# Low-rank products on all rows, a block-diagonal chunk map and shared PSUM banks in the second mixer of a hybrid decoder step

## The chip, the cores and the metric

The kernel runs on one core of a Trainium2 chip. The metric is the device time of one execution in microseconds (us); less is better. The engines are TensorE (PE in the profile; PEld is its weight load), VectorE (DVE), ScalarE (ACT), GpSimd (POOL) and SyncE (SP), whose queue issues the DMAs.

## What is computed

One decoder layer for 512 prompt tokens and 8 x 8 sample tokens (576 columns), all in float32: a first mixer (mLSTM, 4 heads), a second mixer (RWKV-7, 8 heads of 64, in 4 pairs), gates that merge both, a convolutional feed-forward block and a gated embedding. The change lies in the second mixer:

```python
wlog = -jax.nn.softplus(-(lp['r_w0'] + jnp.tanh(wd) @ lp['r_w2'])) - 0.5
decay = jnp.exp(-jnp.exp(wlog.astype(f32)))
a = jax.nn.sigmoid(lp['r_a0'] + ad @ lp['r_a2'])
...
def step(S, inp):
    rt, wt, kt, vt, at, bt = inp
    sa = jnp.einsum('bhij,bhj->bhi', S, at)
    S = S * wt[:, :, None, :] + sa[..., None] * bt[:, :, None, :] + vt[..., None] * kt[:, :, None, :]
    return S, jnp.einsum('bhij,bhj->bhi', S, rt)
```

The kernel computes this recurrence in chunks of 64 tokens: within a chunk by matrix products, and from chunk to chunk by a map of the 64x64 state of each head.

## The kernel before

Activations lie with channels on the 128 partitions and the 576 tokens as columns, in two halves of 288. A dense product (`dense`, L171; its matmul is L190) splits each weight and each activation into a high and a low float32r part and adds three products, so one output tile of 8 input tiles is 2 x 24 matmuls of 128 rows, 128 columns and 288 moving columns. Weights come by `wload` (L158): a DMA from SP into one of 6 staging buffers (L165), a cast on ACT (L166) and a subtraction on DVE (L167) into one of 4 pairs of buffers `wh`, `wl`. A float32r matmul or a transpose leaves one record in the trace, a float32 matmul two.

`PLAN` lists the steps of the two mixers: for each head pair p of the second mixer `rwkv_in` (projections), `rwkv_prep` (L550), `rwkv_mid` (L723), `rwkv_smp` (L839) and `rwkv_out` (L882); the mLSTM heads (`mlstm_head`, L1062); and 16 gate tiles (`gate`). A scheduler then interleaves the instructions of all of these on each engine, with priorities by program order and by a model of times, and writes one fixed order per engine. Each engine takes its order strictly, so a change of a few instructions moves others too. PSUM banks come by tags: "d" (3 banks) for the dense products, "r" (2), "s" (1), "c" (1) and "m" (1) for the mixers.

In the second mixer, per head pair:

- `rwkv_prep` makes decay and gate from two low-rank products, each from a 64-row input. `xw` and `xa` hold 128 rows: the rounded input on one half, its remainder on the other. For each half of the columns and each of the two, L566 multiplies all 128 rows by the rounded weights and L567 the 64 rounded rows by the weights' remainder (`lh`).
- `rwkv_mid` solves the chunks and makes, with 64-row matmuls from one "s" bank at a time: the output within the chunk (L806, a bank for each head), the read maps `Rt` (L817, a bank for each parity of the chunks), the state additions `Ns` (L824), and the transition maps `MT` (L835, again a bank for each parity; L836 adds the identity).
- `rwkv_smp` handles the sample tokens. The values of one head are multiplied with a mask of the 8 sequences (`UVM`, L874, one buffer) and go through one matmul of 512 columns (L876), then the other head.
- `rwkv_out` runs the chain over the chunks: 7 steps, each with two 64x64 matmuls (L902), one for each head on its half of the partitions, and one DVE operation (L903), then the outputs (L909).

After the mixers come the branch products (`gated`, L1229; second mixer's branch first), whose result `mg` goes through w_out. Seven of its eight output tiles have their weights staged by three buffers of their own into `oh`, `ol`; the memory of these tiles is shared with earlier pools.

Of the kernel before, what the change touches and what calls it, by code (L numbers as in the profile page):

```python
# [7 lines left out]
F32 = mybir.dt.float32  # L8
F32R = mybir.dt.float32r
AF = mybir.ActivationFunctionType  # L10
ALU = mybir.AluOpType
# [4 lines left out]
P = 128  # L16
D = 1024
TP = 512
NB = 8
TS = 8  # L20
T = TP + NB * TS
HF = T // 2
# [70 lines left out]
def build(tc, nc, I, O):  # L93
    from contextlib import ExitStack

    V, S, G, TE, SY = nc.vector, nc.scalar, nc.gpsimd, nc.tensor, nc.sync
# [9 lines left out]
    with st0:  # L106
# [263 lines left out]
        with ExitStack() as stn:  # L370
# [156 lines left out]
        NPP = 1  # L527
# [12 lines left out]
            return t.rearrange("g (b x) -> g b x", x=1040)[:, :, 0:1024].rearrange("g b (s y) -> g b s y", y=64)[:, :, :, 0:16]  # L540

        WP = [zeroed(rp, [P, 592], f"WP_{i}", 1.0) for i in range(NPP)]
        YT = [zeroed(rp, [P, 5, P], f"YT_{i}") for i in range(NPP)]

        pairs = [{} for _ in range(4)]
# [4 lines left out]
        def rwkv_prep(p):  # L550
            xr, xk, xv = pairs[p]["x"]
            lr = rp.tile([P, 2, P], F32, tag="t4", name="lr")
            SY.dma_start(lr, I["lora_wa"][:, p])
            lh = rp.tile([P, 3, P], F32R, tag="t5", name="lh")
            S.copy(lh[:, 0:2, :], lr)
            for i in range(2):
                r = slice(64 * i, 64 * i + 64)
                V.tensor_tensor(lh[r, 2, :], lr[r, i, :], lh[r, i, :], ALU.subtract)
            sp = rp.tile([P, T], F32, tag="t1", name="sp")
            tha = rp.tile([P, T], F32, tag="t3", name="tha")  # L560
            for hf in range(2):
                c = slice(hf * HF, (hf + 1) * HF)
                pw, pa = bank("r"), bank("r")
                for i, (pm, x) in enumerate(((pw, xw), (pa, xa))):
                    r = slice(64 * i, 64 * i + 64)
                    TE.matmul(pm[:, 0:HF], lh[:, i, :], x[:, c], start=True, stop=False)  # L566
                    TE.matmul(pm[:, 0:HF], lh[r, 2, :], x[r, c], start=False, stop=True)  # L567
                S.activation(sp[:, c], pw[:, 0:HF], AF.Tanh, bias=hw0[:, p:p + 1], scale=0.5)
                S.activation(tha[:, c], pa[:, 0:HF], AF.Tanh, bias=ha0[:, p:p + 1], scale=0.5)
            V.tensor_scalar(sp, sp, 1.0, None, ALU.add)  # L570
# [16 lines left out]
            pm = bank("r")  # L587
# [131 lines left out]
        def slots(t, inner):  # L719
            a = t[:, 0:1024].rearrange("p (i s x) -> p i s x", i=4, s=4)  # L720
            return (a[:, :, 1:3, :] if inner else a[:, :, 0:4:3, :]), t[:, 1024 + 64 * inner:1024 + 64 * inner + 64]

        def rwkv_mid(p):  # L723
# [74 lines left out]
                V.tensor_copy(At[:, 4 * h:4 * h + 4, :], pu[:, :, 64:128])  # L798

            Y = YT[0]  # L800
            for h in range(2):
                f = slice(64 * h, 64 * h + 64)
                py = bank("s").rearrange("p (i x) -> p i x", i=8)
                for i in range(4):
                    for par in range(2):
                        TE.matmul(py[64 * par:64 * par + 64, i, :], (G0, G1)[par][:, h, i, 64 * par:64 * par + 64], UV[:, 2 * i + par, f], start=True, stop=True)  # L806
                V.tensor_copy(Y[:, 0:4, f], py[:, 0:4, :])
            RT_ = rp.tile([P, 8, 64], F32, tag="Rt", name="Rt")
            RTv = RT_.rearrange("p (i q) x -> p i q x", i=4)
            Rv = slots(AR, 0)[0]  # L810
            for par in range(2):
                b = 64 * (1 - par)
                pm = bank("s").rearrange("p (c x) -> p c x", c=8)
                for i in range(4):
                    for h in range(2):
                        f = slice(64 * h, 64 * h + 64)
                        TE.matmul(pm[f, i, :], At[b:b + 64, 4 * h + i, :], (G0, G1)[par][b:b + 64, h, i, 64 - b:128 - b], start=True, stop=True)  # L817
                V.tensor_tensor(RTv[:, :, par, :], pm[:, 0:4, :], Rv[:, :, par, :], ALU.add)
            WL = wl[:, 0:8].unsqueeze(2).to_broadcast([P, 8, 64])
            pn = bank("s").rearrange("p (c x) -> p c x", c=8)  # L820
            for c in range(8):
# [5 lines left out]
            MT = rp.tile([P, 8, 64], F32, tag="MT", name="MT")  # L827
            MTv = MT.rearrange("p (i q) x -> p i q x", i=4)
            for par in range(2):
                b = 64 * (1 - par)  # L830
                pm = bank("s").rearrange("p (c x) -> p c x", c=8)
                for i in range(4):
                    for h in range(2):
                        f = slice(64 * h, 64 * h + 64)
                        TE.matmul(pm[f, i, :], At[b:b + 64, 4 * h + i, :], BT[b:b + 64, 2 * i + par, f], start=True, stop=True)  # L835
                V.tensor_tensor(MTv[:, :, par, :], pm[:, 0:4, :], cc("ident2", 64).unsqueeze(1).to_broadcast([P, 4, 64]), ALU.add)  # L836
            pairs[p].update(MT=MT, Ns=Ns, RT=RT_, Q4=Q4)

        def rwkv_smp(p):  # L839

            AR, wl, G4, B8, U8, Q4 = (pairs[p][n] for n in ("AR", "wl", "G4", "B8", "U8", "Q4"))
            Y4 = rp.tile([64, P], F32, tag="Y4", name="Y4", bufs=2)
            S0C = rp.tile([P, NB, 64], F32, tag="S0C", name="S0C")
            SY.dma_start(S0C, I["st_S"][p])
            pa = bank("r")
            arv = AR[:, 1024:1152].rearrange("p (s b x) -> p b s x", s=2, b=NB)
            for b in range(NB):
                for h in range(2):
# [12 lines left out]
            for h in range(2):  # L861
                f = slice(64 * h, 64 * h + 64)
                TE.matmul(pu[64:128, f], Q4[64:128, h, :], Xs[64:128, f], start=True, stop=True)
            S.copy(U8[64:128, :], pu[64:128, :])
            py = bank("r")[:, 0:P]
            for h in range(2):
                f = slice(64 * h, 64 * h + 64)
                TE.matmul(py[0:64, f], G4[:, h, 0:64], U8[:, f], start=True, stop=True)
            V.tensor_tensor(Y4, py[0:64, :], Xs[0:64, :], ALU.add)
            pS = bank("r")  # L870
            for h in range(2):
                f = slice(64 * h, 64 * h + 64)
                UVM = rp.tile([P, NB, 64], F32, tag="UVM", name="UVM")
                V.tensor_tensor(UVM, U8[:, f].unsqueeze(1).to_broadcast([P, NB, 64]),  # L874
                                cc("bmask", 8).unsqueeze(2).to_broadcast([P, NB, 64]), ALU.mult)
                TE.matmul(pS[f, :], B8[:, f], UVM, start=True, stop=True)  # L876
            V.tensor_tensor(S0C, S0C, pS.rearrange("p (b x) -> p b x", b=NB), ALU.add)
            V.tensor_tensor(S0C, S0C, wl[:, 8:16].unsqueeze(2).to_broadcast([P, NB, 64]), ALU.mult)
            SY.dma_start(O["o_S_s"][p], S0C)
            pairs[p]["Y4"] = Y4  # L880

        def rwkv_out(p):  # L882
# [14 lines left out]
            V.tensor_copy(Sa[:, 1, :], Ns[:, 0, :])  # L897
            for c in range(1, 8):
                pS = bank("c")
                for h in range(2):  # L900
                    f = slice(64 * h, 64 * h + 64)
                    TE.matmul(pS[f, 0:64], MT[f, c, :], Sa[f, c, :], start=True, stop=True)  # L902
                V.scalar_tensor_tensor(Sa[:, c + 1, :], pS[:, 0:64], wl[:, c:c + 1], Ns[:, c, :], ALU.mult, ALU.add)  # L903
            SY.dma_start(O["o_S_p"][p], Sa[:, 8, :])
            for h in range(2):
# [607 lines left out]
```

## Time and profile before

| | |
|---|---|
| median of 3 runs | 1110.08 us (1108.51 to 1112.6) |
| the profiled execution's own time | 1105.56 us |
| its span, first to last instruction | 1103.9 us |
| granted TensorE clock over the span | 0.995 of full |
| DMA moved | 114.54 MB, 104 GB/s in the mean |

The page gives busy times by engine, the stretches the same by time, and the timeline the start of each matmul. A matmul's duration includes its way through the array, and the next one starts before it ends; the time that it takes from PE's queue is the distance to the next start. Line numbers are those of the kernel before; the kernel after has its own, at most 8 away from these.

### The profile page before, as it was taken

How to read it: one execution, taken by the hardware profiler on the slowest of the kernel's cores; microseconds unless marked ns; L12 is line 12 of the kernel's file. 1: busy time of each engine (PE TensorE's matmuls, PEld its weight loads, DVE VectorE, ACT ScalarE, POOL GpSimd, SP SyncE). 2: the span in 40 equal slices, each digit the busy share in tenths (PEclk: the TensorE clock that was granted, in tenths of full speed). 3: DMA queues.
4: the chain of work that ended last, by engine and by line, in shares of the span. 5: the costliest groups of instructions: out<-in, count | busy, mean ns of one | idle time of the engine just before them, and what ended most of it. 6: DMA issues, size and time to landing. Idle time of an engine off the chain costs nothing. (4 is left out here: it accounts for less than half of the span.)

```text
span 1103.9 us, 23247 instructions
## 1 busy us (share of the span) xinstructions
PE 1075.5 (97%) x9039; PEld 1014.2 (92%) x9039; DVE 785.3 (71%) x1690; ACT 509.2 (46%) x1075; POOL 254.6 (23%) x401
## 2 busy tenths in 40 slices
PE   6899999999999999999989999999999999999997
PEld 5899989989979888898989999999999999999997
DVE  7786756766757667346693799974899569976765
ACT  6584733453435244325241556541455335553732
POOL 6532112220112022002130152410144103510300
PEclk9999999999999999999999999999999999999999
DMA  6343412332342232427780212332223332242414
GB/s 220 96 123 92 105 51 55 97 119 65 93 133 80 75 82 85 141 80 235 231 276 1 69 44 87 96 100 93 77 86 95 93 92 87 84 122 64 147 48 132
DMA packets 90799, 114.54 MB, mean 104 GB/s; under 512 B 35612, under 2 KB 45212, under 8 KB 90688
## 3 DMA queue, kind: packets, MB, share of 16 engines
q1 hardware_dynamic: 90688, 113.05, 34.2%
q8 instruction: 71, 1.16, 0.4%
q14 instruction: 40, 0.33, 0.1%
HBM read 94.57 MB, written 18.45 MB: 102 GB/s over the span
## 5 line engine op out<-in xcount | busy, mean ns | idle before, releaser
L166 ACT CAST wh<-wr 128x512 fp32r<-128x512 f32 (+2 forms) x170 | 101.6, 599 | 198.4 <-PE pd L190 157.3
L167 DVE TENSOR_TENSOR wl<-wr,wh 128x512 fp32r<-128x512 f32 (+2 forms) x170 | 119.7, 707 | 81.2 <-ACT wh L166 78.3
L190 PE MATMUL pd<-actl,wh 128*128 128x288 f32 x384 | 111.9, 295 | 0.0
L190 PE MATMUL pd<-acth,wl 128*128 128x288 f32 x384 | 111.4, 295 | 0.0
L190 PE MATMUL pd<-acth,wh 128*128 128x288 f32 x384 | 110.4, 296 | 0.5 <-ACT pp L1376 0.5
L190 PEld LDWEIGHTS pd<-acth,wh 128*128 128x128 f32 x384 | 71.1, 188 | 0.8 <-ACT pp L1376 0.7
L190 PEld LDWEIGHTS pd<-actl,wh 128*128 128x128 f32 x384 | 71.8, 188 | 0.0
L190 PEld LDWEIGHTS pd<-acth,wl 128*128 128x128 f32 x384 | 71.6, 188 | 0.0
L288 ACT CAST wh<-ws 128x512 fp32r<-128x512 f32 x76 | 47.0, 619 | 47.6 <-PE pd L300 26.8
L289 DVE TENSOR_TENSOR wl<-ws,wh 128x512 fp32r<-128x512 f32 x76 | 59.0, 777 | 8.2 <-ACT wh L288 7.9
L294 POOL TENSOR_TENSOR ws<-wr 128x512 f32<-128x512 f32 x19 | 31.9, 1682 | 93.6 <-DVE wl L289 53.1
L1326 POOL COPY o_f<-u 128x2 f32<-128x2 f32 x22 | 26.6, 1208 | 110.5 <-DVE u L1323 108.8
L288 ACT CAST wh<-wr 128x512 fp32r<-128x512 f32 x57 | 35.3, 619 | 35.0 <-PE pd L300 21.1
L289 DVE TENSOR_TENSOR wl<-wr,wh 128x512 fp32r<-128x512 f32 x57 | 39.6, 694 | 7.3 <-ACT wh L288 7.2
L1335 DVE SCALAR_TENSOR_TENSOR y<-u,vec,y 128x592 f32<-128x592 f32 x44 | 38.0, 863 | 1.4 <-ACT y L1333 1.3
L207 POOL TENSOR_TENSOR rsc<-rsc,nhalf 128x3 f32<-128x3 f32 x8 | 7.3, 912 | 137.0 <-DVE rsc L229 137.0
L247 ACT ACTIVATE sq<-res 128x288 f32<-128x288 f32 x40 | 17.7, 444 | 45.8 <-DVE res L1272 27.2
L190 PE MATMUL pd<-mgl,oh 128*128 128x288 f32 x112 | 33.1, 296 | 0.0
L190 PE MATMUL pd<-mgh,ol 128*128 128x288 f32 x112 | 33.1, 295 | 0.0
L190 PE MATMUL pd<-mgh,oh 128*128 128x288 f32 x112 | 32.8, 295 | 0.0
L1363 DVE TENSOR_TENSOR res<-res,pd 128x288 f32<-128x288 f32 x48 | 20.9, 451 | 15.6 <-PE pd L190 15.5
L190 PE MATMUL pd<-xa0h,wh 128*128 128x288 f32 x86 | 26.6, 310 | 2.1 <-ACT zr L346 2.0
(820 smaller groups left out, 3979.2 us busy)
## 6 DMA issues: line engine op xcount, KB each, us to landing
wr<-i_w_in SPq DMA_DIRECT2D x92, 256.0 KB
wr<-i_f_up SPq DMA_DIRECT2D x88, 256.0 KB
wr<-i_f_down SPq DMA_DIRECT2D x32, 256.0 KB
d_th<-gst SPq DMA_DIRECT2D x16, 288.0 KB
th<-d_th SPq DMA_DIRECT2D x16, 288.0 KB
wr<-i_w_br SPq DMA_DIRECT2D x16, 256.0 KB
wr<-i_w_out SPq DMA_DIRECT2D x16, 256.0 KB
wr<-i_ple_gate SPq DMA_DIRECT2D x16, 256.0 KB
```

The costliest lines, as they stand in the source:

```text
L166: S.copy(wh[:, 0:nk, :], wr[:, 0:nk, :])
L167: V.tensor_tensor(wl[:, 0:nk, :], wr[:, 0:nk, :], wh[:, 0:nk, :], ALU.subtract)
L190: TE.matmul(pm[:, 0:HF], w[:, k % 4, :], a[:, c], start=k == 0 and i == 0, stop=k == n - 1 and i == 2)
L207: G.tensor_tensor(t, t, nhalf[0:t.shape[0], :].to_broadcast([t.shape[0], n]), ALU.pow)
L247: S.activation(sq, x[:, c], AF.Square)
L288: S.copy(wh, w)
L289: V.tensor_tensor(wl, w, wh, ALU.subtract)
L294: e.tensor_tensor(t, a, b, ALU.add)
L1326: G.tensor_copy(o_f[:, j, 0:2], u[:, TP:TP + 2])
L1335: V.scalar_tensor_tensor(y, u[:, i:i + 592], w(i), y, ALU.mult, ALU.add)
L1363: V.tensor_tensor(x1[m][:, c], x1[m][:, c], pss[hf][:, 0:HF], ALU.add)
```

## The change

In `rwkv_prep` the weights' remainder is kept on all 128 rows for both products, and the second matmul of a pair multiplies all 128 rows. In `rwkv_mid` the outputs of both heads go to one bank and leave it in one copy; read and transition maps of one parity share a bank, and the transition maps land in `MTP`, a tile zeroed once, one head's 64x64 map in the upper left and the other's in the lower right of each chunk's 128x128 block. `rwkv_out` then needs one matmul per step. In `rwkv_smp` the mask is applied to both heads in one operation.

```diff
+        MTP = [zeroed(rp, [P, 8, P], f"MT_{i}") for i in range(NPP)]
...
-            lh = rp.tile([P, 3, P], F32R, tag="t5", name="lh")
+            lh = rp.tile([P, 4, P], F32R, tag="t5", name="lh")
             S.copy(lh[:, 0:2, :], lr)
-            for i in range(2):
-                r = slice(64 * i, 64 * i + 64)
-                V.tensor_tensor(lh[r, 2, :], lr[r, i, :], lh[r, i, :], ALU.subtract)
+            V.tensor_tensor(lh[:, 2:4, :], lr, lh[:, 0:2, :], ALU.subtract)
...
                     TE.matmul(pm[:, 0:HF], lh[:, i, :], x[:, c], start=True, stop=False)
-                    TE.matmul(pm[:, 0:HF], lh[r, 2, :], x[r, c], start=False, stop=True)
+                    TE.matmul(pm[:, 0:HF], lh[:, 2 + i, :], x[:, c], start=False, stop=True)
...
+            py = bank("s").rearrange("p (h i x) -> p h i x", h=2, i=4)
             for h in range(2):
                 f = slice(64 * h, 64 * h + 64)
-                py = bank("s").rearrange("p (i x) -> p i x", i=8)
...
-                V.tensor_copy(Y[:, 0:4, f], py[:, 0:4, :])
+            V.tensor_copy(Y[:, 0:4, :].rearrange("p i (h x) -> p h i x", h=2), py)
...
             for par in range(2):
                 b = 64 * (1 - par)
-                pm = bank("s").rearrange("p (c x) -> p c x", c=8)
-                for i in range(4):
-                    for h in range(2):
-                        f = slice(64 * h, 64 * h + 64)
-                        TE.matmul(pm[f, i, :], At[b:b + 64, 4 * h + i, :], (G0, G1)[par][b:b + 64, h, i, 64 - b:128 - b], start=True, stop=True)
-                V.tensor_tensor(RTv[:, :, par, :], pm[:, 0:4, :], Rv[:, :, par, :], ALU.add)
+                pm = bank("s").rearrange("p (q i x) -> p q i x", q=2, i=4)
+                for q, rhs in enumerate((lambda h, i: (G0, G1)[par][b:b + 64, h, i, 64 - b:128 - b],
+                                         lambda h, i: BT[b:b + 64, 2 * i + par, 64 * h:64 * h + 64])):
+                    for i in range(4):
+                        for h in range(2):
+                            TE.matmul(pm[64 * h:64 * h + 64, q, i, :], At[b:b + 64, 4 * h + i, :], rhs(h, i), start=True, stop=True)
+                V.tensor_tensor(RTv[:, :, par, :], pm[:, 0], Rv[:, :, par, :], ALU.add)
+                for h in range(2):
+                    f = slice(64 * h, 64 * h + 64)
+                    V.tensor_tensor(MTv[f, :, par, f], pm[f, 1], cc("ident2", 64)[f].unsqueeze(1).to_broadcast([64, 4, 64]), ALU.add)
...
+            UVM = rp.tile([P, NB, P], F32, tag="UVM", name="UVM")
+            V.tensor_tensor(UVM, U8.unsqueeze(1).to_broadcast([P, NB, P]), cc("bmask", 8).unsqueeze(2).to_broadcast([P, NB, P]), ALU.mult)
             for h in range(2):
                 f = slice(64 * h, 64 * h + 64)
-                UVM = rp.tile([P, NB, 64], F32, tag="UVM", name="UVM")
...
-                TE.matmul(pS[f, :], B8[:, f], UVM, start=True, stop=True)
+                TE.matmul(pS[f, :], B8[:, f], UVM[:, :, f], start=True, stop=True)
...
             for c in range(1, 8):
                 pS = bank("c")
-                for h in range(2):
-                    f = slice(64 * h, 64 * h + 64)
-                    TE.matmul(pS[f, 0:64], MT[f, c, :], Sa[f, c, :], start=True, stop=True)
+                TE.matmul(pS[:, 0:64], MT[:, c, :], Sa[:, c, :], start=True, stop=True)
```

The scheduler's order changes with it. On PE, in the chain of the last head pair, a step before and a step of the change (L902, now L894: the chain's matmul; L909, now L901: an output; L1100 and L1080: matmuls of the last mLSTM head):

```order
L190 MATMUL pd<-xa1l,wh 128x288
L190 MATMUL pd<-xa1h,wl 128x288
L902 MATMUL pm<-Sa,MT 64x64 x2
L909 MATMUL pm<-Sa,Rt 64x64
L190 MATMUL pd<-xa2h,wh 128x288
L190 MATMUL pd<-xa2l,wh 128x288
```

```order
L190 MATMUL pd<-xa7l,wh 128x288
L190 MATMUL pd<-xa7h,wl 128x288
L894 MATMUL pm<-Sa,MT_719 128x64
L901 MATMUL pm<-Sa,Rt 64x64
L1080 MATMUL pm<-Mrow,selr 128x512
L190 MATMUL pd<-xa0h,wh 128x288
```

Two small matmuls have become one of full size, and the lone output product behind it stays small. On DVE, at the first head pair's read maps (L818, now L820), the transition adds (L823 of the change) now follow at once; L655, now L654, masks the next pair's scores, L167 is a weight split, and hsc and hr belong to an mLSTM head's norm:

```order
L1148 SCALAR_TENSOR_TENSOR hr<-mv,hsc 128x4
L818 TENSOR_TENSOR Rt<-pm,AR 128x4x64
L655 TENSOR_TENSOR G_1657<-pm,cst 128x512 x2
L167 TENSOR_TENSOR wl<-wr,wh 128x512
L818 TENSOR_TENSOR Rt<-pm,AR 128x4x64
```

```order
L654 TENSOR_TENSOR G_1654<-pm,cst 128x512 x2
L1136 TENSOR_TENSOR hsc<-hsc,mv 128x4
L820 TENSOR_TENSOR Rt<-pm,AR 128x4x64
L823 TENSOR_TENSOR MT_719<-pm,cst 64x4x64 x2
L1137 TENSOR_SCALAR hsc<-hsc 128x4
L167 TENSOR_TENSOR wl<-wr,wh 128x512
```

A weight split now stands behind three evacuations of one bank. On SP's queue, at the end of the mixers, before (o_C_s is the store of the last mLSTM head's sample state, th a gate tile, res an input tile of the residual):

```order
L165 DMA wr<-i_w_br 128x512
L1196 DMA o_C_s<-C_6004 128x1032
L1232 DMA th<-d_th_88 128x576
L165 DMA wr<-i_w_br 128x512
L1232 DMA th<-d_th_73 128x576
L165 DMA wr<-i_w_br 128x512
L1232 DMA th<-d_th_75 128x576
L165 DMA wr<-i_w_out 128x512 x3
```

and of the change:

```order
L165 DMA wr<-i_f_up 128x512
L1258 DMA res_6709<-i_x 128x576
L1224 DMA th<-d_th_81 128x576
L165 DMA wr<-i_f_up 128x512
L1258 DMA res_6710<-i_x 128x576
L1188 DMA o_C_s<-C_5954 128x1032
L1224 DMA th<-d_th_83 128x576
L165 DMA wr<-i_f_up 128x512
L1258 DMA res_6711<-i_x 128x576
L165 DMA wr<-i_w_out 128x512
L1224 DMA th<-d_th_85 128x576
L165 DMA wr<-i_w_out 128x512 x2
```

The store has moved behind the loads of six more gate tiles, and with it most of the w_out loads; on PE the last matmuls of that state (L1193, now L1185) stand 144 dense products ahead of the first use of `oh` instead of 284.

## Rows read from the trace of the kernel before

**Rows 1.** The page's first part: busy time, share of the span, instructions of an engine.

```profile
PE 1075.5 (97%) x9039; PEld 1014.2 (92%) x9039; DVE 785.3 (71%) x1690; ACT 509.2 (46%) x1075; POOL 254.6 (23%) x401
```

**Rows 2.** Stretches of the span: busy us of each engine (instructions), granted clock, DMA share, GB/s.

```profile
60.00:500.00 440.00, 439.61 (x4368) 388.67 (x4367) 282.16 (x706) 194.84 (x458) 81.53 (x173) 1.00 0.32 91
500.00:580.00 80.00, 75.70 (x533) 72.07 (x532) 61.07 (x112) 34.53 (x64) 18.73 (x19) 0.98 0.76 249
```

**Rows 3.** Waits of 60 to 500 us, PE: engine line, waited for, us, times, longest.

```profile
PE pm L760 <- DMA TT<-scr0t: 0.4, 1, 0.4
```

**Rows 4.** Timeline of PE: start us, us, engine, line, operation, out<-in, weights, moving, count.

```profile
132.30 0.29 PE L190 MATMUL pd<-xa6h,wl 128*128 128x288 f32 x1
132.44 0.29 PE L566 MATMUL pm<-xa,lh 128*128 128x288 f32 x1
132.66 0.39 PE L567 MATMUL pm<-xa,lh 64*128 64x288 f32 x1
132.98 0.40 PE L190 MATMUL pd<-xa7h,wh 128*128 128x288 f32 x1
133.22 0.29 PE L190 MATMUL pd<-xa7l,wh 128*128 128x288 f32 x1
```

**Rows 5.** The same timeline: a run of 16 small records between dense products.

```profile
180.14 0.29 PE L190 MATMUL pd<-xa7l,wh 128*128 128x288 f32 x1
180.36 0.68 PE L817 MATMUL pm<-G,At 64*64 64x64 f32 x16
180.97 0.40 PE L190 MATMUL pd<-xa7h,wl 128*128 128x288 f32 x1
181.21 0.29 PE L190 MATMUL pd<-xa4h,wh 128*128 128x288 f32 x1
```

**Rows 6.** The same timeline: 32 records on column halves in turn.

```profile
187.04 1.15 PE L824 MATMUL pm<-UV,BT 128*64 128x64 f32 x32
188.12 0.48 PE L645 MATMUL pm<-AR,BK 64*128 64x128 f32 x2
```

**Rows 7.** The same timeline: full-size transposes, then one chain step, between dense products.

```profile
208.98 0.60 PE L700 MATMUL pm<-cst,AR 128*128 128x128 f32 x4
209.34 0.38 PE L190 MATMUL pd<-xa1h,wl 128*128 128x288 f32 x1
209.55 0.30 PE L190 MATMUL pd<-xa2h,wh 128*128 128x288 f32 x1
...
209.82 0.29 PE L190 MATMUL pd<-xa2h,wl 128*128 128x288 f32 x1
210.04 0.33 PE L902 MATMUL pm<-Sa,MT 64*64 64x64 f32 x4
210.31 0.40 PE L190 MATMUL pd<-xa3h,wh 128*128 128x288 f32 x1
210.54 0.30 PE L190 MATMUL pd<-xa3l,wh 128*128 128x288 f32 x1
```

**Rows 8.** The same timeline: the masked product of one head.

```profile
227.89 1.07 PE L876 MATMUL pm<-UVM,B 128*64 128x512 f32 x2
228.89 0.40 PE L190 MATMUL pd<-xa6h,wh 128*128 128x288 f32 x1
```

**Rows 9.** The same timeline: records on one half of the columns.

```profile
159.50 1.76 PE L1117 MATMUL pm<-C,QM 128*64 128x129 f32 x14
```

**Rows 10.** Line 836: count, duration ns min/median/max, first and last start, form.

```profile
L836 DVE TENSOR_TENSOR MT<-pm,cst x8: 411/421/424, 193.9 to 463.5; 128x256 f32<-128x256 f32 x8
```

**Rows 11.** Tile YT on POOL: its memset, columns as before.

```profile
L457 POOL MEMSET YT<- x1: 629/629/629, 50.6 to 50.6; 128x640 f32 x1
```

**Rows 12.** Tile oh, 540 to 620 us: the weights of the output projection.

```profile
L190 PE MATMUL pd<-mgh,oh x97: 290/294/297, 576.4 to 619.8; 128*128 128x288 f32 x97
L166 ACT CAST oh<-wr x14: 602/620/626, 546.5 to 577.6; 128x512 fp32r<-128x512 f32 x14
```

More of the change, by code (lines that the diff above doesn't have):

```diff
@@ L564, in rwkv_prep @@
                 for i, (pm, x) in enumerate(((pw, xw), (pa, xa))):
-                    r = slice(64 * i, 64 * i + 64)
                     TE.matmul(pm[:, 0:HF], lh[:, i, :], x[:, c], start=True, stop=False)
-                    TE.matmul(pm[:, 0:HF], lh[r, 2, :], x[r, c], start=False, stop=True)
+                    TE.matmul(pm[:, 0:HF], lh[:, 2 + i, :], x[:, c], start=False, stop=True)
                 S.activation(sp[:, c], pw[:, 0:HF], AF.Tanh, bias=hw0[:, p:p + 1], scale=0.5)
@@ L800, in rwkv_mid @@
             Y = YT[0]
+            py = bank("s").rearrange("p (h i x) -> p h i x", h=2, i=4)
             for h in range(2):
                 f = slice(64 * h, 64 * h + 64)
-                py = bank("s").rearrange("p (i x) -> p i x", i=8)
                 for i in range(4):
                     for par in range(2):
-                        TE.matmul(py[64 * par:64 * par + 64, i, :], (G0, G1)[par][:, h, i, 64 * par:64 * par + 64], UV[:, 2 * i + par, f], start=True, stop=True)
-                V.tensor_copy(Y[:, 0:4, f], py[:, 0:4, :])
+                        TE.matmul(py[64 * par:64 * par + 64, h, i, :], (G0, G1)[par][:, h, i, 64 * par:64 * par + 64], UV[:, 2 * i + par, f], start=True, stop=True)
+            V.tensor_copy(Y[:, 0:4, :].rearrange("p i (h x) -> p h i x", h=2), py)
             RT_ = rp.tile([P, 8, 64], F32, tag="Rt", name="Rt")
@@ L810, in rwkv_mid @@
             Rv = slots(AR, 0)[0]
+            MT = MTP[0]
+            MTv = MT.rearrange("p (i q) x -> p i q x", i=4)
             for par in range(2):
                 b = 64 * (1 - par)
-                pm = bank("s").rearrange("p (c x) -> p c x", c=8)
-                for i in range(4):
-                    for h in range(2):
-                        f = slice(64 * h, 64 * h + 64)
-                        TE.matmul(pm[f, i, :], At[b:b + 64, 4 * h + i, :], (G0, G1)[par][b:b + 64, h, i, 64 - b:128 - b], start=True, stop=True)
-                V.tensor_tensor(RTv[:, :, par, :], pm[:, 0:4, :], Rv[:, :, par, :], ALU.add)
+                pm = bank("s").rearrange("p (q i x) -> p q i x", q=2, i=4)
[8 more added lines that the diff above has]
+                    V.tensor_tensor(MTv[f, :, par, f], pm[f, 1], cc("ident2", 64)[f].unsqueeze(1).to_broadcast([64, 4, 64]), ALU.add)
             WL = wl[:, 0:8].unsqueeze(2).to_broadcast([P, 8, 64])
@@ L826, in rwkv_mid @@
             V.tensor_tensor(Ns, pn, WL, ALU.mult)
[L827 to L832, printed above, removed]
-                    for h in range(2):
-                        f = slice(64 * h, 64 * h + 64)
-                        TE.matmul(pm[f, i, :], At[b:b + 64, 4 * h + i, :], BT[b:b + 64, 2 * i + par, f], start=True, stop=True)
-                V.tensor_tensor(MTv[:, :, par, :], pm[:, 0:4, :], cc("ident2", 64).unsqueeze(1).to_broadcast([P, 4, 64]), ALU.add)
             pairs[p].update(MT=MT, Ns=Ns, RT=RT_, Q4=Q4)
@@ L870, in rwkv_smp @@
             pS = bank("r")
+            UVM = rp.tile([P, NB, P], F32, tag="UVM", name="UVM")
+            V.tensor_tensor(UVM, U8.unsqueeze(1).to_broadcast([P, NB, P]), cc("bmask", 8).unsqueeze(2).to_broadcast([P, NB, P]), ALU.mult)
             for h in range(2):
                 f = slice(64 * h, 64 * h + 64)
-                UVM = rp.tile([P, NB, 64], F32, tag="UVM", name="UVM")
-                V.tensor_tensor(UVM, U8[:, f].unsqueeze(1).to_broadcast([P, NB, 64]),
-                                cc("bmask", 8).unsqueeze(2).to_broadcast([P, NB, 64]), ALU.mult)
-                TE.matmul(pS[f, :], B8[:, f], UVM, start=True, stop=True)
+                TE.matmul(pS[f, :], B8[:, f], UVM[:, :, f], start=True, stop=True)
             V.tensor_tensor(S0C, S0C, pS.rearrange("p (b x) -> p b x", b=NB), ALU.add)
@@ L899, in rwkv_out @@
                 pS = bank("c")
-                for h in range(2):
-                    f = slice(64 * h, 64 * h + 64)
-                    TE.matmul(pS[f, 0:64], MT[f, c, :], Sa[f, c, :], start=True, stop=True)
+                TE.matmul(pS[:, 0:64], MT[:, c, :], Sa[:, c, :], start=True, stop=True)
                 V.scalar_tensor_tensor(Sa[:, c + 1, :], pS[:, 0:64], wl[:, c:c + 1], Ns[:, c, :], ALU.mult, ALU.add)
```

## The prediction

> **What bounds the kernel now.** I read the page's busy times first, then the stretches, then TensorE's waits, then its timeline. TensorE (PE) is busy for 97% of the span [rows 1]. That alone proves little, since pipelined matmuls overlap, so the stretches come next: from 60 to 500 us, where the mixers run, PE is busy 439.61 of 440 us at a granted clock of 1.00 (the 2.4 GHz level), VectorE (DVE) 282 and ScalarE 195 [rows 2]. In those 440 us PE waits once, for 0.4 us [rows 3]. So what ends last there is PE's own queue, and a microsecond taken out of that queue leaves the span, as long as no new wait takes its place. What must be priced is therefore the distance between matmul starts, not their durations.
>
> The timeline gives that distance. Two plain dense products start 0.13 us apart: 132.30 to 132.44 [rows 4]. Where a matmul of another tile form is put between them, three things are lost: it starts 0.22 us after the last dense product (180.14 to 180.36), the run takes its own time, and the second dense product behind it starts 0.24 us after the first instead of 0.13 [rows 5].
>
> **Low-rank products.** Of the two matmuls of a pair the second (L567) uses 64 rows, the first and all dense products 128. From the last dense product to the second one behind the pair it takes 132.30 to 133.22, 0.92 us [rows 4]; four starts at 0.13 would be 0.53. With 128 rows in both nothing is left of the difference, 0.39 us. There are 16 such pairs (four head pairs, two halves, two gates): 6.2 us. About six of them follow other small-tile work, where a tenth stays: 5.6. Lower bound 0.28 each if the late second dense product stays, 4.5.
>
> **Shared banks.** A run of 16 small records costs 180.14 to 181.21 less two dense starts, 0.80 us [rows 5]. A run of 32 takes 1.08 us from its start to the next, against 0.61 for 16 [rows 6, 5], so it costs 1.27. Two runs made one save 0.33. Per head pair the output products go from two runs to one, the read and transition maps from four to two: twelve unions, 4.0 us. In the order of the change a 64-row run of the next head pair's score matmuls now often stands on both sides of a union (the third run of the same block had one side), which costs a border of up to 0.2 us; and some of the old runs leaned on other small work. I take 3.0, bounds 1.5 and 4.0.
>
> **State chain.** Each of 28 steps issues two 64x64 matmuls on the diagonal (four records); now one 128x128 (two records). Between dense products a step costs 209.82 to 210.54 less two starts, 0.45 us. Nothing in this trace is a full-size fp32 matmul with 64 moving columns; the nearest are full-size transposes, four of which cost 208.98 to 209.55 less one start, 0.44, so two cost 0.22 [rows 7]. That saves 0.23 where dense work stands around it. But inside small-tile company the old step had no border and the new one has two. In the order of the change 12 steps go straight back into dense work (2.8 us saved), 7 are followed by a lone 64x64 output product, which now pays the border that both shared (about 0), and 9 touch small runs (0.2 lost each, 1.8). Sum 1.0; bounds 3 us lost (the 0.1 that a 128-column record takes beyond a small one, 28 times) and 6.4 gained (28 times 0.23).
>
> **Masked values.** The two heads' masked products (L876), 512 columns each, now stand next to each other, on the two halves of the columns. One of them takes 227.89 to 228.89, 1.00 us [rows 8]. Side by side they take between 1.0 (both halves work at once) and 2.0 us (one after the other, only a border of 0.2 saved). The rows on halves in turn decide: 32 records of 64 columns take 1.08 us [rows 6], 0.53 ns a column, while 14 records of 129 columns all on one half take 1.76 [rows 9], 0.97 ns a column. So the halves overlap, but PE starts in order: the first head's second record waits for its first, and only then can the second head start. I take three half-microsecond slots for four, 0.7 us saved with the border, times four: 2.8, bounds 0.8 and 4.8. The Trainium skill (TensorEngine Tiling, Tiling Modes) says that different tiles load and multiply in parallel; by it alone this term would be 4.8 and the sum 2 us larger. The trace agrees for 64 columns in turn; for 512 no run here shows it.
>
> **What is added elsewhere.** The identity is now added per head: 16 DVE instructions instead of 8, 0.42 us each [rows 10], 3.4 us more on DVE; two masked products of 512 columns become one of 1024. DVE has 158 us free in the stretch [rows 2], and in the order at least 12 dense products or as much other PE work (1.6 us) stand between a bank's matmuls and the next user of that bank, more than the 1.3 us of three adds, so I cost it at nothing; without that cover it would be 8 times 0.85, 7 us. The new zeroed tile is a POOL memset of 1024 columns, about 1.0 us by the 0.63 us of 640 [rows 11]; it delays POOL's copies near 51 us behind a queue of 58 dense products (8 us): nothing, at most 1.
>
> **The end of the mixers.** The planner's new order moves the last mLSTM head: its final sample-state matmuls stand 284 dense products ahead of the output projection's first tile from w_out's staged loads before, 144 now. The queue of loads shows the same: the store of that state comes only behind six th loads, two f_up and two w_out loads more, and the other w_out loads behind it. So those loads may run 140 times 0.13, some 18 us, later against PE. Now their casts run from 546.5 to 577.6, 14 in 31 us, and the projection starts to use them at 576.4 [rows 12]. Moved by 18 they begin near 564.5, so the first staged output tile has its two with 7 us to spare; the last one needs all 14 six tiles of 24 products later, at about 595.5, and they end near 595.6. The cover is just used up. I take 1.4 us of new waits, bounds 0 and 5.
>
> **Sum.** 5.6 + 3.0 + 1.0 + 2.8 − 1.4 = 11.0 us. The profiled execution took 1105.56 us (span 1103.9 and 1.7 around it), 0.4% under the median 1110.08, so against its own time the change gives 1094.6. The saving is an amount of PE work, not a share; from the median it gives 1099.0 us, 1.0% less. I forecast faster. This forecast's own range, from the bounds of its terms met half-way, is 1094 to 1103.
>
> **Rivals.**
> First, the chain loses and the masked products don't overlap. A full-size map loads 128 columns for 64 moving ones; four small records of the old step fit into 0.27 us, four full-size ones into 0.36 [rows 7]. Then the chain costs 3 us instead of giving 1, the masked products give 0.8: 11.0 − 4.0 − 2.0 = 5.0, 1105.1 us. The Trainium skill (TensorE: Matmul & The Clock Gate, Step-by-step: what each phase is for) has weight loads grow with the number of columns and not of rows, which speaks for this rival and against the block-diagonal map. Against it stand the borders of rows 7, which the small form pays and the full one doesn't.
> Second, the late w_out loads. If the first of them comes 7 us later than assumed, the last lands 7 us after PE wants it, and PE stands for all of it: 12.4 − 7 = 5.4, 1104.7 us. For it: the DMA share of 0.76 at 249 GB/s from 500 to 580 us [rows 2]. Against: the 2.2 us a load of rows 12 were set by a DVE that was also needed by the gated products, and would shorten without them.
> Third, the low-rank pairs don't do what they should: if the distance behind L567 comes from switching banks and not from its 64 rows, 5.6 us stay, and 1104.7 us results.
> Fourth, slower: DVE takes over as releaser in the mixers. The merged evacuations (Rt, then two transition adds) and the one masked product wait on PE results in DVE's fixed order, and the weight splits (L167) stand behind them. Four pairs of weight buffers of 24 products each, three of them ahead, are the cover, up to 10 us of dense work; from the point where DVE's waits have used that up, PE stops. If the 28 changed DVE instructions then held it up by 0.6 us each, 17 us would be eaten, 6 more than the 11 gained: 1116 us. Against: PE waited for none of them in 440 us [rows 3].
>
> **Chances.** Forecast 0.62, first rival 0.15, second 0.11, third 0.06, fourth 0.06. A measurement of this kernel tells about 0.5%, 5.6 us, from no change. Faster by more than that: the forecast and nearly half of the first three rivals, 0.77. Within it: 0.17. Slower: 0.06. The range that leaves out two in ten reaches from 1090 (masked products 4.8, chain 4, unions 4, no wait) to 1107, which takes in the first three rivals.
>
> **What would show it.** PE's timeline: L565 and L566 0.13 us apart and no 64-row form among them; read and transition maps as one run of 32 records, 1.1 us; a chain step between dense products at 0.22 us; the two masked products in 1.5 us. PE's waits in the mixers still under 2 us. The prediction is wrong if PE's waits there grow by over 5 us, if waits for w_out's tiles appear after 560 us, or if the busy stretch is not shorter by about 12 us.

## The result and the profile after

The changed kernel takes 1089.03 us (median of 4 runs, 1087.62 to 1096.89); the kernel before, run beside it, 1109.3 (4 runs). The ratio is 0.9848, 95% interval [0.9816, 0.9881], about 17 us less (13 to 20; the two medians themselves lie 20.3 apart). Forecast were 1099.0, range 1090 to 1107: the direction was right, the gain of 11.0 us too small, and the time lies 1 us below the range. The profiled executions say the same, spans of 1103.9 and 1087.8 us, 16.1 less.

Lines of the changed kernel are named by its own numbers: L565 and L566 are the low-rank pair, L819 the maps, L894 the chain step, L901 its output product, L870 the masked products, L759 the products with TT (L760 before). The busy times (the page's first part), against [rows 1]:

```profile
PE 1061.6 (98%) x8983; PEld 1015.3 (93%) x8983; DVE 780.0 (72%) x1686; ACT 508.7 (47%) x1075; POOL 264.1 (24%) x402
```

The saving is PE time: 13.9 of 16.1 us are PE's busy time. To split it, I take the stretch from the first low-rank product to the first use of `oh`. The windows view of before and of after over it (length, then busy time and records of PE, PEld, DVE, ACT, POOL, the granted clock, DMA share and GB/s):

```profile
63.09:576.41 513.32, 508.63 (x4848) 454.06 (x4847) 338.96 (x812) 225.00 (x515) 99.99 (x188) 1.00 0.39 116
```

```profile
63.40:560.75 497.35, 494.12 (x4792) 454.51 (x4791) 330.12 (x802) 220.18 (x508) 104.41 (x188) 1.00 0.39 115
```

All but 0.1 us of the gain lies here: 513.3 to 497.4. Three parts make it up. PE's idle time falls from 4.7 to 3.2 us. A stretch of 3.4 us at a granted clock of 0.5 (1.2 GHz), which before had from 515.0 us on, right after PE stood for the last mLSTM head's norm and the branch's first input, is gone. Its price shows in the timeline of before, where dense products there start 0.24 us apart and not 0.13:

```profile
515.14 0.44 PE L190 MATMUL pd<-y0h,wl 128*128 128x288 f32 x1
515.38 0.44 PE L190 MATMUL pd<-y1h,wh 128*128 128x288 f32 x1
515.62 0.44 PE L190 MATMUL pd<-y0l,wh 128*128 128x288 f32 x1
```

In 3.4 us stand 14 such products that take 1.9 us at full clock, so it cost 1.5. What is left, 13.0 us, is PE's own work. PE's waits in the stretch, before and after (waiting line and what it waited for; us, times, longest). L1235, now L1227, is where DVE takes a branch product out of its bank into `ya`; `og` is the last mLSTM head's output, `wh` a weight cast, `sp` the tanh of the first gates, `TT` the inverses of the chunks' blocks:

```profile
PE pd L190 <- DVE ya L1235: 3.1, 5, 1.0
PE pm L1157 <- DVE og L1155: 0.8, 1, 0.8
...
PE pd L190 <- ACT y0h L195: 0.2, 1, 0.2
```

```profile
PE pd L190 <- DVE ya L1227: 1.0, 1, 1.0
PE pm L759 <- DMA TT<-scr1t: 0.9, 1, 0.9
PE pd L190 <- ACT wh L166: 0.8, 1, 0.8
PE pm L565 <- ACT sp L567: 0.5, 1, 0.5
```

No wait for w_out's tiles appears. PE's timeline of the changed kernel (start, us, engine, line, form, count) shows the parts, a low-rank pair, a union of maps, a lone chain step, and one with its output product:

```profile
131.22 0.29 PE L190 MATMUL pd<-xa6h,wl 128*128 128x288 f32 x1
131.35 0.29 PE L565 MATMUL pm<-xa,lh 128*128 128x288 f32 x1
131.48 0.30 PE L566 MATMUL pm<-xa,lh 128*128 128x288 f32 x1
131.62 0.29 PE L190 MATMUL pd<-xa7h,wh 128*128 128x288 f32 x1
131.75 0.29 PE L190 MATMUL pd<-xa7l,wh 128*128 128x288 f32 x1
...
175.55 0.29 PE L190 MATMUL pd<-xa0l,wh 128*128 128x288 f32 x1
175.78 0.68 PE L819 MATMUL pm<-G,At 64*64 64x64 f32 x16
176.29 0.63 PE L819 MATMUL pm<-BT,At 64*64 64x64 f32 x16
176.86 0.40 PE L190 MATMUL pd<-xa0h,wl 128*128 128x288 f32 x1
177.09 0.30 PE L190 MATMUL pd<-xa1h,wh 128*128 128x288 f32 x1
...
288.43 0.29 PE L190 MATMUL pd<-xa5l,wh 128*128 128x288 f32 x1
288.56 0.33 PE L894 MATMUL pm<-Sa,MT 128*128 128x64 f32 x2
288.70 0.38 PE L190 MATMUL pd<-xa5h,wl 128*128 128x288 f32 x1
288.91 0.29 PE L190 MATMUL pd<-xa6h,wh 128*128 128x288 f32 x1
...
461.24 0.29 PE L190 MATMUL pd<-xa2l,wh 128*128 128x288 f32 x1
461.37 0.33 PE L894 MATMUL pm<-Sa,MT 128*128 128x64 f32 x2
461.63 0.32 PE L901 MATMUL pm<-Sa,Rt 64*64 64x64 f32 x2
461.88 0.40 PE L190 MATMUL pd<-xa2h,wl 128*128 128x288 f32 x1
462.12 0.29 PE L190 MATMUL pd<-xa3h,wh 128*128 128x288 f32 x1
```

The pair is invisible now: four starts 0.13 apart, 0.53 us where [rows 4] had 0.92. The lone step costs 288.43 to 288.91 less two starts, 0.22 (before 0.45, [rows 7]), the union 1.08 from its start to the next dense product and 1.27 in all. These are the prediction's figures to 0.01 us. The masked products are not:

```profile
218.37 1.08 PE L870 MATMUL pm<-UVM,B 128*64 128x512 f32 x4
219.38 0.27 PE L901 MATMUL pm<-Sa,Rt 64*64 64x64 f32 x1
```

All four records take 1.01 us, as long as two of one head took [rows 8]. The records start at 218.37, 218.38, 218.85 and 218.85: the second head does not wait for the first head's second record. At the other three head pairs the four take 1.01 to 1.07 us.

### The profile page after: what moved, and what is told of

Its sections match the earlier page's. It is cut to its first block, busy times and chain, and to the rows that moved or that the text cites. A ratio compares the mean times of both kernels' runs of the same rounds, so it can differ in the third digit from the quotient of the medians.

```text
span 1087.8 us, 23134 instructions
## 1 busy us (share of the span) xinstructions
PE 1061.6 (98%) x8983; PEld 1015.3 (93%) x8983; DVE 780.0 (72%) x1686; ACT 508.7 (47%) x1075; POOL 264.1 (24%) x402
## 4 chain that ended last, share of the span: by engine, by line
PE 86%; DVE 5%; DMA 4%; ACT 2%; issue 1%; POOL 0%; SPq 0%; POOLq 0%; DVEq 0%; ACTq 0%
PE pd L190 51%; PE pd L300 19%; PE pm L644 1%; DMA wr<-i_w_out 1%; PE pm L1119 1%; PE pm L819 1%; DVE xnf L262 1%; PE pm L793 1%; PE pm L1185 1%; PE pm L1109 1%; DMA wr<-i_f_up 1%; PE pm L1092 1%; DVE wl L167 1%; PE pm L901 1%; PE pm L759 0%
## 5 line engine op out<-in xcount | busy, mean ns | idle before, releaser
L166 ACT CAST wh<-wr 128x512 fp32r<-128x512 f32 (+2 forms) x170 | 101.7, 600 | 191.5 <-PE pd L190 162.9
L167 DVE TENSOR_TENSOR wl<-wr,wh 128x512 fp32r<-128x512 f32 (+2 forms) x170 | 115.9, 685 | 85.6 <-ACT wh L166 84.1
```

Of the source, the lines that this page charges most:

```text
L166: S.copy(wh[:, 0:nk, :], wr[:, 0:nk, :])
L167: V.tensor_tensor(wl[:, 0:nk, :], wr[:, 0:nk, :], wh[:, 0:nk, :], ALU.subtract)
```

## The experiments

The ratio is to the kernel before, run beside each (medians of 1105.3 to 1106.7 us, for the change 1109.3). A distance between two rows, neither of them before, carries the errors of both ratios, 3 to 5 us. The next columns come from the one profiled execution of each kernel, over the same stretch as above: its length, PE's idle time in it, the time at half clock, and PE's own work, which is the length less the idle time less 1.5 us for each 3.4 us at half clock.

| kernel | ratio, 95% | length | idle | half clock | own work |
|---|---|---|---|---|---|
| before | 1 | 513.3 | 4.7 | 3.4 | 507.1 |
| the change | 0.9848 [0.9816, 0.9881] | 497.4 | 3.2 | 0 | 494.1 |
| lowrank_alone | 0.9952 [0.9931, 0.9972] | 508.4 | 6.1 | 0 | 502.3 |
| masked_alone | 0.9966 [0.9952, 0.9981] | 511.7 | 6.6 | 3.4 | 503.6 |
| chain_alone | 1.0027 [1.0014, 1.0040] | 518.1 | 7.2 | 3.4 | 509.4 |
| banks_alone | 0.9990 [0.9970, 1.0010] | 517.1 | 8.9 | 10.2 | 503.7 |
| before_reordered | 1.0076 [1.0051, 1.0102] | 526.5 | 10.7 | 13.6 | 509.8 |
| after_reordered | 0.9901 [0.9875, 0.9926] | 503.0 | 5.6 | 3.4 | 495.9 |
| no_chain | 0.9899 [0.9866, 0.9932] | 498.9 | 3.6 | 3.4 | 493.8 |
| same_half | 0.9948 [0.9925, 0.9971] | 506.7 | 5.3 | 6.8 | 498.4 |
| before_reordered_tt | 0.9990 [0.9977, 1.0003] | 510.1 | 3.2 | 0 | 506.9 |
| pad_store | 0.9847 [0.9822, 0.9873] | 496.2 | 4.2 | 0 | 492.0 |
| pad_tt | 0.9830 [0.9813, 0.9847] | 493.6 | 4.2 | 0 | 489.4 |
| after_tt | 0.9910 [0.9892, 0.9928] | 500.1 | 2.1 | 3.4 | 496.5 |

**One part of the change at a time.** The theory: the four terms of the sum, the masked one at 4.8 us, and a stand (PE waiting) before the branch products that the new order removed. The rivals are in the expectations.

```diff
-                    TE.matmul(pm[:, 0:HF], lh[r, 2, :], x[r, c], start=False, stop=True)
+                    TE.matmul(pm[:, 0:HF], lh[:, 2 + i, :], x[:, c], start=False, stop=True)
```

> Of the change only the low-rank products on all 128 rows. Theory from the trace of the change (a two-pair block there takes 0.52 us beyond its neighbours' dense starts where it took 1.31): 16 pairs at 0.39, so 6 us less than before (5.6 in the prediction). Rival 3 of the prediction (the distance comes from the bank, not from 64 rows): 0. The last mLSTM head's norm still stands ahead of the first branch product on PE, so the stand there (wait of 0.8 us, half clock for 3.4 us, 3.1 us of waits for ya) should stay as before, if that order is what made it go.

Measured: 5.3 us less (3.1 to 7.6), 4.8 of it PE's own work. Rival 3 is out. The waits stayed, 0.8 us for `og` at 511 us and 3.5 for `ya` from 552 to 569 us, but the half clock behind the first did not come, so a stand there and a half clock do not always go together.

```diff
-                UVM = rp.tile([P, NB, 64], F32, tag="UVM", name="UVM")
+            UVM = rp.tile([P, NB, P], F32, tag="UVM", name="UVM")
```

> Of the change only the mask on both heads at once, so that the two 512-column products stand side by side. Both column halves at work at once: four records in 1.0 us, 4.8 us less than before in all. In-order slots, as the prediction took it: 1.5 us for four records, 2.8 less. One after the other: 2.0 us, 0.8 less. The order at the end of the mixers is as before, so no gain there.

Measured: 3.8 less (2.1 to 5.3). The records stand as in the whole change, four in 1.0 us, so the first case holds for them. The 4.8 us are not seen in full: own work fell by 3.5, and PE's idle time grew by 1.9.

```diff
-                    TE.matmul(pS[f, 0:64], MT[f, c, :], Sa[f, c, :], start=True, stop=True)
+                TE.matmul(pS[:, 0:64], MT[:, c, :], Sa[:, c, :], start=True, stop=True)
```

> Of the change only the block-diagonal transition maps with one full-size matmul a step. Prediction: 1.0 us less; rival 1: 3 us more. From the trace of the change a lone step takes 0.22 us beyond dense starts (0.45 before) but a step with its output product 0.62 (0.51 before), so I now expect 0 to 2 less in the mixers. The last head's norm comes 8 dense products after the first branch product instead of ahead of it: if the stand at that place goes by the order, up to 1 us more is gained.

Measured: 3.0 us more (1.5 to 4.4). That is rival 1's number for the chain, and my new expectation missed. The trace shows two sources: 2.5 us more of idle time, of which waits for TT make 1.3 (1.7 us against 0.4), and 2.3 us more of own work.

```diff
-                pm = bank("s").rearrange("p (c x) -> p c x", c=8)
+                pm = bank("s").rearrange("p (q i x) -> p q i x", q=2, i=4)
```

> Of the change only the shared banks (outputs of both heads in one, read and transition maps of a parity in one). Prediction for the runs that merge: 3.0 us less (1.5 to 4.0). Here the order moves the last mLSTM head's norm 68 dense products behind the first branch product, as the whole change does with 112. If that order is what took away the stand before the branch products, 2.5 to 3.5 us more are gained, 5.5 to 6.5 in all, with the half clock near 515 us gone; if the end of the mixers has nothing to do with it, 3.0 in all and the half clock stays.

Measured: 1.1 less, interval from 3.3 less to 1.1 more. Neither case: the half clock near 515 us is gone, as said, but three others came (320, 395 and 415 us), and waits for TT of 3.9 us. PE's own work fell by 3.4, the prediction's 3.0.

The four alone save 7 us together, the whole change 17. By own work it is 9.4 us (4.8, 3.5, 3.4 and a loss of 2.3) against 13.0, so the larger part of what is missing lies in waits and clock, and 3.6 us of own work stay unexplained. The next question was what a new order by itself is worth.

**The same instructions in another order.** The state additions (`Ns`) are emitted on the other side of the maps, in before and in the changed kernel:

```diff
+            MT = rp.tile([P, 8, 64], F32, tag="MT", name="MT")
...
             WL = wl[:, 0:8].unsqueeze(2).to_broadcast([P, 8, 64])
...
-            MT = rp.tile([P, 8, 64], F32, tag="MT", name="MT")
```

> The kernel before with the state additions emitted behind the transition maps instead of ahead of them: the same instructions, but the scheduler's order on every engine changes. If what the single parts lost (10 us more together than the whole change) comes from the waits that a new order happens to have, this one too moves by several us, between 3 less and 6 more, by PE's waits and stretches at half clock, and TensorE's work between its waits stays at 508.6 us from the first low-rank product to the first use of oh (within 1). If order costs nothing, within 1 us of before.

Measured: 8.4 us more (5.6 to 11.3), above what I expected. Not one instruction is added. PE's waits over the stretch, and its timeline at the longest:

```profile
PE pm L760 <- DMA TT<-scr1t: 5.1, 4, 2.3
PE pd L190 <- DVE ya L1235: 3.4, 5, 1.0
```

```profile
222.51 0.28 PE L902 MATMUL pm<-Sa,MT 64*64 64x64 f32 x2
224.52 0.33 PE L760 MATMUL pm<-TT,X 64*64 64x64 f32 x2 [1.73 <-DMA TT<-scr1t]
225.21 1.97 PE L760 MATMUL pm<-TT,X 64*64 64x64 f32 x30 [0.37 <-DMA TT<-scr1t]
```

PE stands for TT, and from 224.8 on the granted clock is 0.5 for 6.8 us; the 32 records take 1.97 us for 30 where a full clock gives 32 in 1.1. The same follows at 409.2. Own work should have stayed; it reads 2.7 us higher, so a difference of that size in the column says little by itself.

> The changed kernel with the state additions emitted ahead of the maps: the same instructions in another order. If the changed kernel's few waits (2.8 us from the first low-rank product to the first use of oh, no half clock in it) are luck of its order, this one has 5 to 10 us of them, as three of the four single parts have, and takes 1091 to 1097 us. If the change itself removes waits, it takes 1089 again, within 1.5.

Measured: 0.9901, 5.8 us behind the change. TensorE waits 2.4 us for TT and a half clock comes at 311 us, so the lack of these in the change is its order's. The waits for `ya` stay low (1.1 us), as in the change.

**Where the wait comes from.** TT goes out to memory and comes back in another layout. SP's queue in before_reordered (start, duration, DMA):

```profile
216.21 0.32 SPq L739 DMA_DIRECT2D scr1q<-Qd  x1
216.62 0.60 SPq L738 DMA_DIRECT2D scr1t<-Td  x1
220.09 1.28 SPq L749 DMA_DIRECT2D Q<-scr1q  x2
221.46 1.26 SPq L746 DMA_DIRECT2D TT<-scr1t  x2
```

Qd is ready 0.4 us before Td and goes first, so Q's loads, which nobody needs yet, stand ahead of TT's. The edit makes Q the later one:

```diff
             SY.dma_start(blocks16(st_), Td)
-            SY.dma_start(blocks16(sq_), Qd)
+            Qc = rp.tile([72, 16, 16], F32, tag="prd", name="Qc")
+            G.tensor_copy(Qc, Td.rearrange("q t s -> q s t"))
+            SY.dma_start(blocks16(sq_), Qc)
```

> The reordered kernel before, and in it the transposed block inverses (Td, read back as TT) stored ahead of Qd, which is first copied by POOL, so that SP issues the loads of TT ahead of those of Q. Theory: what the reordered kernel lost (11.6 us against the kernel before) is TensorE's wait for TT (5.1 us in the trace, four times) and the stretches at half clock behind it (twice 6.8 us, about 3 us each). Sooner by some 1.3 to 2 us, the waits for TT fall under 1.5 us, no half clock near 225 and 409 us, and the time is 1105 to 1111. Rival: the waits only move to another load or to the order's next stand, and it stays within 3 us of 1117.

Measured: 0.9990, 9.5 us less than without the edit. SP's queue at the same head pair, and all of PE's waits over the stretch:

```profile
212.11 0.32 SPq L738 DMA_DIRECT2D scr1t<-Td  x1
212.80 0.33 SPq L741 DMA_DIRECT2D scr1q<-Qc  x1
214.72 1.28 SPq L748 DMA_DIRECT2D TT<-scr1t  x2
```

```profile
PE pd L190 <- DVE ya L1237: 2.6, 4, 1.0
PE pm L762 <- DMA TT<-scr0t: 0.6, 1, 0.6
```

From Td's store to TT's load it is 2.6 us, not 4.8; the waits for TT fall from 5.1 to 0.6 and no half clock is left in the stretch. The edit changes the order too, so that all 9.5 us are TT's is not shown; that its waits and their half clock went is.

**The masked products on one half.** Second head's product into the first head's half:

```diff
-                TE.matmul(pS[f, :], B8[:, f], UVM[:, :, f], start=True, stop=True)
+                TE.matmul(pS[0:64, :], B8[:, f], UVM[:, :, f], start=True, stop=True)
```

> The changed kernel, but both masked products write the first head's half of the columns, so the second overwrites the first, and only that half is added to the states of the sample sequences (the second head's state sum is left out, the first's is replaced). If the four records ran in 1.0 us because they lie on two halves of the columns, they take 2.0 us here, each 0.5 behind the other: 4 us more of TensorE's time for four head pairs, 1093, plus or minus the luck of the order. If they overlap for another reason, 1.0 us again.

Measured: 1100.85 us, and in PE's timeline

```profile
219.34 1.93 PE L870 MATMUL pm<-UVM,B 128*64 128x512 f32 x4
221.20 0.27 PE L901 MATMUL pm<-Sa,Rt 64*64 64x64 f32 x1
```

Four records take 1.86 us in place of 1.01, with weights, columns and neighbours alike: where the output lies is the cause. (Both products then write not only the same half but the same place in it; no run takes the two apart.) Four head pairs make 3.4 us; own work grew by 4.3. Of the rest of the 11 us the trace shows 3.0 as 6.8 us at half clock and 2.1 as idle time.

**The chain taken back.**

```diff
-                TE.matmul(pS[:, 0:64], MT[:, c, :], Sa[:, c, :], start=True, stop=True)
+                for h in range(2):
+                    f = slice(64 * h, 64 * h + 64)
+                    TE.matmul(pS[f, 0:64], MT[f, c, :], Sa[f, c, :], start=True, stop=True)
```

> The changed kernel with the state chain as it was before: transition maps of 64 columns and two 64x64 matmuls a step (the identity added for both heads at once). From the blocks of thirteen traces a full-size step costs 0.27 us and a step of four small records 0.32, so TensorE's own work grows by 28 times 0.05, 1.3 us. That is less than what another order is worth: the reordered changed kernels lost 6 to 7 us. So 1090 to 1098, with what exceeds 1.3 us in PE's waits and in stretches at half clock. If it stays under 1089, the block-diagonal map costs time; if TensorE's busy time between the first low-rank product and the first use of oh grows by over 4 us without half clock, the map is worth more than the blocks say.

Measured: 0.9899, 5.6 us behind the change, with 1.6 us of wait for TT and a half clock at 222 us; own work 0.3 below the change's. The blocks are the stretches of PE between dense products; a least-squares fit of their lengths to the records in them gave the prices that the expectation quotes. By it the map saves 1.3 us, alone it cost 2.3, here 0.3: its own worth stays open, within what the column can tell of zero.

**A better version.** The mLSTM heads' sample states have the same pairs of a 128-row and a 64-row matmul, 16 of them, at 0.62 us beyond dense starts:

```diff
-                for i, (v, r) in enumerate(((vh, P), (vl, 64))):
+                for i, (v, r) in enumerate(((vh, P), (vl, P))):
...
-                    TE.matmul(pc[:, 0:258], ks[0:(P, 64)[i], :], m, start=i == 0, stop=i == 1)
+                    TE.matmul(pc[:, 0:258], ks, m, start=i == 0, stop=i == 1)
```

> The changed kernel, and in the mLSTM heads' sample-state products the same edit as in the low-rank products: the second matmul of each of 16 pairs, of 64 rows, now takes all 128, with the remainder of the values on both halves (which also adds the product of the two remainders). A pair takes 0.62 us beyond the dense starts around it; two full-size float32r matmuls of 258 columns should take about 0.24. 16 times 0.38 is 6 us less than the changed kernel, 1083, if the order stays as good; 0 if the price of the pair lies in its bank or its 258 columns. The order's luck can take back up to 6.

Measured: 0.9847, no gain on the change. A pair between dense products costs what was expected:

```profile
314.25 0.29 PE L190 MATMUL pd<-xa1h,wh 128*128 128x288 f32 x1
314.39 0.40 PE L1186 MATMUL pm<-VS 128*128 128x258 f32 x2
314.62 0.30 PE L190 MATMUL pd<-xa1l,wh 128*128 128x288 f32 x1
314.76 0.29 PE L190 MATMUL pd<-xa1h,wl 128*128 128x288 f32 x1
```

314.25 to 314.76 less two starts is 0.24. But only 9 of the 16 pairs of the changed kernel stood between dense products alone, and own work fell by 2.1 us, not 6. Other places took that back: the first low-rank product starts 1.4 us later, the wait for the first gates' `sp` is 1.3 us and not 0.5, the one for a weight cast 1.2 and not 0.8.

> The padded kernel (second matmul of the sample-state pairs on all rows) with TT stored and loaded ahead of Q. In the padded kernel's own trace TensorE waited for TT nowhere by more than 0.3 us; its 4.3 us of waits lie at tanh's half of the first gates, at a weight cast, at the branch. So TT itself gives nothing here; what changes is the order: between 1083 (the padded pairs' 6 us seen at last) and 1095. If the padded pairs' gain was not eaten by waits but is not there, 1089 or more.

Measured: 1087.33 us, 0.9830. The lowest time of the study, 19 us under before, but its interval overlaps the change's. Own work is 4.7 us under the change's, still not 6, and this order has a wait of 1.3 us for TT.

> The changed kernel with TT stored and loaded ahead of Q: its one wait for TT (0.9 us) goes, 1088 to 1089 if the order stays as good; by the order's luck up to 7 us more, as in the reordered changed kernel.

Measured: 0.9910, 6.9 us behind the change. The wait for TT is gone as expected; the time is at the far end of the range left to the order, with a half clock at 317.5 us and own work 2.4 us higher.

## Why the prediction was right in direction and too small

**Low-rank products: right.** 0.39 us a pair seen, 5.3 us alone against 5.6 forecast.

**Shared banks: right.** 1.27 us a union seen, own work 3.4 us less alone against 3.0. Alone, waits and half clock took most of it back.

**State chain: size not settled.** The lone step measured 0.22 as forecast. The step with an output product, entered at about 0, lost 0.1 (0.62 in the timeline above; a step with its output cost 0.46 to 0.57 before). The sum of 1.0 cannot be told from zero.

**Masked values: mis-sized.** The step that failed is "PE starts in order: the first head's second record waits for its first, and only then can the second head start". The second head started 0.01 us after the first. Counted as the prediction counts, the term is 4.0 us from the records alone and up to 4.8 with the borders, not 2.8; masked_alone's own work fell by 3.5. The Trainium skill (TensorEngine Tiling, Tiling Modes) has different tiles load and multiply in parallel, by which the prediction had put the sum 2 us higher. The trace agrees with it, with 1.01 us on two halves against 1.86 on one.

**End of the mixers: wrong sign.** The loads did come later: w_out's casts began 11.8 us ahead of their first use, as forecast (12), where before they were 29.9 ahead. The tile `oh`'s casts (L166) and splits (L167) in the changed kernel, first and last start:

```profile
L166 ACT CAST oh<-wr x14: 602/620/624, 549.0 to 573.4; 128x512 fp32r<-128x512 f32 x14
L167 DVE TENSOR_TENSOR ol<-wr,oh x14: 676/692/767, 549.7 to 574.0; 128x512 fp32r<-128x512 f32 x14
```

They ran in 24.4 us, not in the 31 of [rows 12]; the prediction named that chance and did not take it. So no wait for them came. The step that failed is "I take 1.4 us of new waits": it priced the later loads only as inputs that PE may have to wait for. But their splits run on DVE, and so does `ya`, which empties the banks of the branch products. The windows view of the last 25 us ahead of the first use of `oh`, before and after (DVE's is the third busy time):

```profile
551.41:576.41 25.00, 21.88 (x157) 20.72 (x156) 24.98 (x36) 12.79 (x22) 9.06 (x5) 1.00 0.88 290
```

```profile
535.75:560.75 25.00, 23.27 (x169) 22.56 (x170) 19.98 (x33) 10.61 (x18) 9.03 (x5) 1.00 0.86 275
```

Before, DVE is busy for 24.98 of 25 us there and PE waits 3.1 us for `ya`; after, it is 19.98 and 1.0. All fourteen traces divide this way. In the change and the six kernels built on it the casts begin 9 to 12 us ahead of that use, DVE is busy for 18.5 to 20.0 us and PE waits 0.9 to 1.6 for `ya`; in before and the six built on it the casts begin 18 to 31 us ahead, DVE is busy for 22.7 to 25.0 and PE waits 2.6 to 4.0. No run moves the loads alone, so that they are the cause is argued from these traces, not shown.

The norm of the last head, no longer in front of the branch products, is the other part: before, PE stood there 0.8 us for `og` and 0.2 for the branch's first input, and then ran at half clock (1.5). With the 2.1 for `ya` that is 4.6 us; against it stand 1.8 more of waits for TT, a weight cast and `sp`. So waits and clock gave 3.0 us (by the lengths, unrounded) where a loss of 1.4 was entered, 4.4 of the 5 us missing.

**The sum.** Own work: 12.4 forecast, 13.0 measured. That close an agreement is partly luck: the masked values were 1.2 to 2.0 too small, the chain's gain of 1.0 was not seen, the four parts alone make 9.4, and one order against another moves the column by 2.7. Distances between starts times counts gave the single prices to 0.01 us (the masked values aside) and the total as well as it can be read.

**What the range lacked** is a term for the order: the same instructions emitted in another sequence took 8.4 us (before) and 5.8 us (change) more. The forecast knew that the order changes, looked for one wait at one place, and gave the rest nothing. Of the 16 us some 13 are work and 3 are waits and clock; the 2.1 for `ya` came with the change in every order tried, the rest with an order that happens to stand little. Three kernels within 2.5 us of the change's own work (after_reordered, no_chain, after_tt) are 5.6 to 6.9 us slower. The range's ends are also not the sums they are said to be: the terms named for 1090 (5.6, 4, 4, 4.8, no wait) make 18.4 us, 1091.7, and the bounds met half-way on the slow side give 1105, not 1103. And the 0.97 ns a column of [rows 9] comes from a duration, 1.76 us; those records start 0.111 us apart, 0.86 ns a column, which changes nothing in the term.

**Rivals.** Of the first, the masked products one after the other are out by the halves; its loss of 3 us by the chain is what chain_alone measured, and no_chain did not find it again, so that half stays open. The second is out by the casts, the third by lowrank_alone; the fourth: DVE released PE for 1.0 us in the stretch (ya), less than before.

## What to carry to other kernels

Where a scheduler fixes the order, price PE work by distances between starts, and enter the order as a term of its own (here it was worth 6 to 8 us) before believing a difference of that size; re-emit the same instructions once to see it. Fill up a 64-row matmul that stands among full-size ones (0.39 us each here), and put products on the two column halves next to each other. Where PE waits for a round trip through memory, look at what stands ahead of its load on the queue: the later of two stores was the urgent one. And where a transfer comes later, ask not only who waits for it but which engine its follow-up work leaves free in the meantime.

## What the runs showed of the chip that was not expected

Two products of 512 columns on the two column halves run fully at once, record by record (1.01 against 1.86 us on one half). A half clock came without a stand: in after_tt PE was busy for all of 300 to 317.5 us, from 314.0 to 316.6 almost only with records of 32x32 and of 2 columns, and after six dense products more the granted clock was 0.5 for 3.4 us; and in lowrank_alone a stand of 0.8 us at 511 us brought none.
